# Down projection of a decoder block's FFN: from 528 plain matmuls to Strassen's seven products in two rounds

## The chip, the cores and the metric

The kernel runs on one core of one Trainium2 chip. The metric is the device time of one execution in microseconds, as the median of several runs of the same program. A run's time is a little more than the span of its profile, which goes from the first to the last instruction. The core has five engines that run beside each other, each through its own list of instructions in order: PE (matrix multiply), DVE (vector), ACT (scalar and activation functions), POOL (general purpose) and SP, which here issues DMAs. PE writes to PSUM, which has eight banks of 128 x 512 fp32.

## What is computed

One decoder block on 512 tokens of width 1024 in fp32: a mixing half (sliding-window attention beside a gated linear recurrence, merged by gates), then a SwiGLU FFN with 2816 hidden columns, each behind an RMS norm, and a last RMS norm. The change is in the FFN:

```python
u = rmsnorm(h, norm_ffn_g[layer])
z = (jax.nn.silu(jnp.einsum('bsd,df->bsf', u, w_ffn_gate[layer]))
     * jnp.einsum('bsd,df->bsf', u, w_ffn_up[layer]))
h = h + jnp.einsum('bsf,fd->bsd', z, w_ffn_down[layer])
return rmsnorm(h, norm_final_g)
```

## The kernel before, in words

**Arithmetic.** Every large product is done in three matmuls. Each operand is split into a high part, which is the value rounded to the type fp32r, and a low part, the rest; the product is high by high, high by low and low by high, summed in PSUM (lines 367 to 369 for projections, 886 for the down projection).

**Weights.** The class `Weights` (lines 41 to 117) streams all weights in one list of units. A unit is 1 MB: a tile `raw` of 128 x 2048, of which there are two buffers. Each unit makes two granules, `wh` and `wl` of 128 x 1024, with three buffers each. `split` has ACT copy a granule's high part (line 103) and DVE subtract it from the raw weights for the low part (line 107). `get` hands out the next granule and has the two behind it split. A raw buffer is loaded anew, through SP's queue, when the last subtraction that reads it is done.

**Before the FFN.** The output projection adds into `hn`, the residual stream: 4 token tiles of 128 rows by 1024 columns in SBUF (line 818). `hn` is transposed on PE into the PSUM tiles `px` (line 821), from which ACT and DVE make `u2h` and `u2l`, the split and transposed input of the FFN.

**Gate and up.** For each of the 11 pairs p of hidden tiles f (128 columns each) there are two gate products and two up products, each of 24 matmuls of 512 columns (tokens) into a PSUM tile `ps_f`. DVE multiplies the gate with the row scale `R` (line 855), ACT takes the sigmoid, POOL multiplies (lines 859 and 860), DVE multiplies the up product with the result to `zz` (line 865). ACT and DVE split it into `zh` and `zl` (lines 866 and 867). `R` itself comes from a small product into `ps_bc`, once, behind the first gate product (lines 255 to 261).

**Down.** For each of the 22 hidden tiles f, `z` of four token tiles is multiplied with the 128 x 1024 weights of f, into eight PSUM banks (two halves of 512 columns for each token tile). For the first 18 f the loop is over f, then token tiles. The weights of the last four f are all split ahead, and then the loop is over token tiles first: a token tile's sums are complete before the next one's last matmuls. So the end of row tile t (lines 897 to 929) runs beside the matmuls of t + 1: DVE adds `hn` (`residual`, line 907), ACT squares and sums, POOL multiplies by `gfin`, DVE reduces, POOL takes the power -0.5, ACT and DVE scale, and two DMAs write the row out.

**Order.** The program is recorded with a tile framework that puts each engine's instructions in an order of its own by a plan of when their inputs will be there; the order in the source is not always that of the engine. All waits are on semaphores.

Of the kernel before, what the change touches and what calls it, by code (L numbers as in the profile page):

```python
# [22 lines left out]
P = 128  # L23
# [10 lines left out]
TAIL_F = 4  # L34
# [6 lines left out]
class Weights:  # L41
# [13 lines left out]
    def load(self, u):  # L55
# [4 lines left out]
        if kind == "f":  # L60
# [23 lines left out]
    def split(self, i, pool=None, bufs=3, high=None, low=None, low_after=None):  # L84
# [5 lines left out]
        if kind == "c":  # L90
            src = raw.rearrange("p (k n) -> p k n", k=KD)[:, :, half * P:(half + 1) * P]
            shape = dict(k=KD)
        else:
            n = {"k": 256, "n": 512, "f": 1024}[kind]
            src = raw[:, half * 1024:(half + 1) * 1024].rearrange("p (k n) -> p k n", n=n)
            shape = dict(n=n)
        pool = pool or self.pool
        h = pool.tile([P, 1024], F32R, tag="wh", bufs=bufs, name=f"wh{i}")
        l = pool.tile([P, 1024], F32R, tag="wl", bufs=bufs, name=f"wl{i}")
        hv = h.rearrange("p (k n) -> p k n", **shape)  # L100
        lv = l.rearrange("p (k n) -> p k n", **shape)
# [7 lines left out]
        self.done = i + 1  # L109

# [10 lines left out]
def block_kernel(ctx: ExitStack, tc: tile.TileContext, x, norm_mix_g, w_in, b_in,  # L121
# [47 lines left out]
    for p in range(NF // 2):  # L169
        units += [("c", w_g, 256 * p), ("c", w_u, 256 * p)]  # L170
    units += [("f", w_d, 2 * p) for p in range(NF // 2)]
# [22 lines left out]
    reset = cst.tile([P, S], F32, name="reset")  # L194
    dve.memset(reset, 1.0)
    dve.memset(reset.rearrange("p (a b) -> p a b", b=64)[:, :, 0:1], 0.0)
    low_m = low.bitcast(U32).unsqueeze(1).broadcast_to([P, NT, P])
    up_m = up.bitcast(U32).unsqueeze(1).broadcast_to([P, NT, P])
# [39 lines left out]
    hib = cst.tile([P, D], F32, name="hib")  # L238
# [9 lines left out]
    uh = upool.tile([P, KD, S], F32R, name="uh")  # L248
    ul = upool.tile([P, KD, S], F32R, name="ul")
# [4 lines left out]

    def row_broadcast(dst, col, sp):
        diag = sp.tile([P, NT, P], F32, tag="diag", name="diag")
        for t in range(NT):
            dve.tensor_scalar(diag[:, t, :], ident, col[:, t:t + 1], None, ALU.mult)
        ps = ps1([P, S], "ps_bc")
        pe.matmul(ps, ones, diag.rearrange("p t c -> p (t c)"), start=True, stop=True)  # L260
        dve.tensor_copy(dst, ps)
# [574 lines left out]

    zpool = newpool("z", "right")
    fp = newpool("f", "right")
    zh = zpool.tile([P, NF, S], F32R, name="zh")
    zl = zpool.tile([P, NF, S], F32R, name="zl")  # L840

    def fproject(then=None):
        wh, wl = W.get(limit=len(W.grans) - 1 - TAIL_F)
        ps = psb([P, S], "ps_f")
        run(mm3(ps, wh, wl, u2h, u2l))
        if then:
            then()
        return ps

    for p in range(NF // 2):  # L850
        gs = []
        for a in range(2):
            zg = fp.tile([P, S], F32, tag="zg", bufs=2, name="zg")
            first = p == 0 and a == 0
            tt(zg, fproject((lambda: row_broadcast(R, rstd2, u2pool)) if first else None),  # L855
               R, ALU.mult)
            sg = fp.tile([P, S], F32, tag="sg", bufs=2, name="sgf")
# [3 lines left out]
            gs.append(zg)  # L861
        for a in range(2):
            f = 2 * p + a
            z = fp.tile([P, S], F32, tag="z", bufs=2, name="zz")
            tt(z, fproject(), gs[a], ALU.mult)  # L865
            act(zh[:, f, :], z, AF.Copy)
            tt(zl[:, f, :], z, zh.bitcast(F32)[:, f, :], ALU.subtract)
# [8 lines left out]
    acc0 = ps2([P, 2, S], "acc0")  # L876
    acc = [[acc0[:, 0, :], acc0[:, 1, :]],
           [ps1([P, S], "acc1"), ps1([P, S], "acc1")],
           [ps1([P, S], "acc2"), psb([P, S], "acc2")],
           [psb([P, S], "acc3"), psb([P, S], "acc3")]]  # L880

    def down(t, f, wh, wl, halves):
        ts = slice(t * P, (t + 1) * P)
        for ah, wv in ((zh, wh), (zh, wl), (zl, wh)):
            for half in halves:
                pe.matmul(acc[t][half], ah[:, f, ts], wv[:, 0, half * S:half * S + S],  # L886
                          start=f == 0 and ah is zh and wv is wh,
                          stop=f == NF - 1 and ah is zl)

    for f in range(NF - TAIL_F):  # L890
        wh, wl = W.get(limit=len(W.grans) - 1 - TAIL_F)
        for t in range(NT):
            down(t, f, wh, wl, (0, 1))
    first = len(W.grans) - TAIL_F
    for i in range(first, len(W.grans)):
        W.split(i, wd, TAIL_F)
    for t in range(NT):
        y = dp.tile([P, D], F32, tag="y", bufs=2, name="yo")
        jk = dp.tile([P, D], F32, tag="jk", bufs=1, name="jkd")
        s2 = dp.tile([P, 5], F32, tag="s2", bufs=2, name="s2d")  # L900
        dve.memset(s2[:, 4:5], EPS)

        def residual(half):
            for c in (2 * half, 2 * half + 1):
                cs = slice(c * 256, c * 256 + 256)
                o = (c % 2) * 256
                tt(y[:, cs], acc[t][half][:, o:o + 256], hn[:, t, cs], ALU.add)
                act(jk[:, cs], y[:, cs], AF.Square, scale=1.0 / 32.0,
                    accum_out=s2[:, c:c + 1])

        for half in range(2):
            for f in range(NF - TAIL_F, NF):
                down(t, f, *W.ready[first + f - (NF - TAIL_F)], (half,))
            if t:
                residual(half)
        if not t:
# [48 lines left out]
```

## Time and profile before

| | |
|---|---|
| median of 3 runs | 909.62 us (909.52 to 909.93) |
| profiled execution, its own time | 909.4 us |
| its span | 907.7 us |
| granted PE clock, mean | 0.999 |
| busy: PE, DVE, ACT, POOL | 896.5, 461.1, 368.2, 141.8 us |
| moved by DMA | 85.71 MB, mean 94 GB/s |
| stretch of the down projection's matmuls | 781.0 to 900.7 us |

In the profile's rows PE is the matmul, PEld its weight load, and L886 is line 886 of the kernel. A group's row has the line, the engine, the operation, what it writes and reads with the shapes, the number of instructions, then busy us and the mean ns of one, then the engine's idle time before them and what ended it. A row in order of time has start and length in us. A row of the table of windows has the stretch and its length, busy us with the number of instructions for PE, PEld, DVE, ACT and POOL, then the granted clock, the share of DMA and GB/s.

### The profile page before, as it was taken

To read this page: it belongs to the slowest core of one execution; us is meant where nothing else is said; L and a number is where in the kernel's file an instruction comes from. 1 tells how busy PE (TensorE), PEld (TensorE's weight loads), DVE (VectorE), ACT (ScalarE), POOL (GpSimd) and SP (SyncE) were. 2 spreads that over 40 slices of the span, in tenths; PEclk is the share of its full clock that TensorE was granted. 3 is DMA by queue.
4 is the path that set the end of the run, shared out by engine and by line. 5 is a ranking of instruction groups with operands and counts; after the bars stand their busy time and mean duration, and the time that the engine had idled before them with its cause. 6 is when DMAs were issued, how large, how long until landed. Compare 5 with 4: busy or idle time off the path is not lost.

```text
span 907.7 us, 11182 instructions
## 1 busy us (share of the span) xinstructions
PE 896.5 (99%) x4476; PEld 758.5 (84%) x4476; DVE 461.1 (51%) x717; ACT 368.2 (41%) x618; POOL 141.8 (16%) x148
## 2 busy tenths in 40 slices
PE   8999999999999999999999999999999999999996
PEld 7888889888898988888888887888888888888885
DVE  5677877647484755745335345344433344322314
ACT  6566765655453545215232333233222233211214
POOL 3013533300000000000000002222333322100004
PEclk9999999999999999999999999999999999999999
DMA  7221311222221141322243222222223333322212
GB/s 257 94 94 47 94 47 47 94 93 94 93 90 50 47 140 47 94 92 93 94 160 118 94 93 93 93 94 93 93 93 96 106 109 107 116 93 93 93 47 93
DMA packets 71472, 85.71 MB, mean 94 GB/s; under 512 B 1690, under 2 KB 64252, under 8 KB 71420
## 3 DMA queue, kind: packets, MB, share of 16 engines
q1 hardware_dynamic: 70828, 83.95, 28.5%
q10 hardware_dynamic: 592, 1.05, 0.3%
q8 instruction: 35, 0.57, 0.3%
q14 instruction: 17, 0.14, 0.0%
HBM read 82.90 MB, written 2.10 MB: 94 GB/s over the span
## 4 chain that ended last, share of the span: by engine, by line
PE 97%; SPq 1%; DMA 0%; DVE 0%; POOL 0%; ACT 0%; issue 0%; POOLq 0%; DVEq 0%
PE acc L886 13%; PE ps_big L367 13%; PE ps_big L369 13%; PE ps_big L368 13%; PE ps_f L368 9%; PE ps_f L369 9%; PE ps_f L367 9%; PE ps_v L378 2%; PE ps_v L379 2%; PE ps_v L377 2%; PE ps_o L379 2%; PE ps_o L378 2%; PE ps_o L377 2%; PE pv L503 1%; PE sc L447 1%; PE po L662 1%
## 5 line engine op out<-in xcount | busy, mean ns | idle before, releaser
L103 ACT ACTIVATE wh<-raw 128x1024 fp32r<-128x1024 f32 x147 | 155.1, 1059 | 401.3 <-PE ps_f L368 159.7
L107 DVE TENSOR_TENSOR wl<-raw,wh 128x1024 fp32r<-128x1024 f32 x147 | 180.5, 1230 | 163.7 <-ACT wh L103 163.5
L367 PE MATMUL ps_big<-uh,wh 128*128 128x512 f32 x376 | 148.8, 396 | 0.0
L368 PE MATMUL ps_big<-ul,wh 128*128 128x512 f32 x376 | 147.8, 393 | 0.0
L369 PE MATMUL ps_big<-uh,wl 128*128 128x512 f32 x376 | 147.7, 393 | 0.0
L368 PE MATMUL ps_f<-u2l,wh 128*128 128x512 f32 x352 | 137.5, 391 | 0.1
L367 PE MATMUL ps_f<-u2h,wh 128*128 128x512 f32 x352 | 137.0, 390 | 0.2 <-ACT u2h L134 0.2
L369 PE MATMUL ps_f<-u2h,wl 128*128 128x512 f32 x352 | 136.9, 389 | 0.0
L369 PEld LDWEIGHTS ps_big<-uh,wl 128*128 128x128 f32 x376 | 70.7, 188 | 14.2
L368 PEld LDWEIGHTS ps_big<-ul,wh 128*128 128x128 f32 x376 | 70.8, 188 | 13.6
L367 PEld LDWEIGHTS ps_big<-uh,wh 128*128 128x128 f32 x376 | 70.7, 188 | 13.5
L368 PEld LDWEIGHTS ps_f<-u2l,wh 128*128 128x128 f32 x352 | 66.1, 188 | 14.4 <-DVE u2l L827 0.5
L367 PEld LDWEIGHTS ps_f<-u2h,wh 128*128 128x128 f32 x352 | 66.0, 188 | 14.0 <-ACT u2h L134 0.5
L369 PEld LDWEIGHTS ps_f<-u2h,wl 128*128 128x128 f32 x352 | 66.1, 188 | 13.9 <-issue 0.2
L859 POOL TENSOR_TENSOR zg<-zg,sgf 128x512 f32<-128x512 f32 x22 | 39.4, 1794 | 162.6 <-ACT sgf L139 162.6
L886 PE MATMUL acc<-wh,zl 128*128 128x512 f32 x176 | 57.0, 389 | 0.0
L886 PE MATMUL acc<-wl,zh 128*128 128x512 f32 x176 | 56.9, 389 | 0.0
L886 PE MATMUL acc<-wh,zh 128*128 128x512 f32 x176 | 56.8, 389 | 0.0
L865 DVE TENSOR_TENSOR zz<-ps_f,zg 128x512 f32<-128x512 f32 x22 | 15.2, 692 | 66.4 <-PE ps_f L369 62.7
L855 DVE TENSOR_TENSOR zg<-ps_f,R 128x512 f32<-128x512 f32 x22 | 15.1, 691 | 62.6 <-PE ps_f L369 62.6
L253 POOL TENSOR_TENSOR r<-ss,neghalf 128x4 f32<-128x4 f32 x8 | 10.1, 1260 | 232.8 <-DVE ss L252 232.8
L886 PEld LDWEIGHTS acc<-wh,zh 128*128 128x128 f32 x176 | 33.0, 188 | 6.9
(222 smaller groups left out, 1478.1 us busy)
## 6 DMA issues: line engine op xcount, KB each, us to landing
raw<-in_w_in_dram SPq DMA_DIRECT2D x27, 1024.0 KB, 5.1
raw<-in_w_ffn_gate_dram SPq DMA_DIRECT2D x11, 1024.0 KB, 5.9
raw<-in_w_ffn_up_dram SPq DMA_DIRECT2D x11, 1024.0 KB, 5.2
raw<-in_w_ffn_down_dram SPq DMA_DIRECT2D x11, 1024.0 KB, 4.9
raw<-in_w_branch_attn_dram SPq DMA_DIRECT2D x4, 1024.0 KB, 5.3
raw<-in_w_branch_hgrn_dram SPq DMA_DIRECT2D x4, 1024.0 KB, 4.8
raw<-in_w_out_dram SPq DMA_DIRECT2D x4, 1024.0 KB, 5.5
xt<-in_x_dram SPq DMA_DIRECT2D x4, 512.0 KB, 6.5
```

The costliest lines, as they stand in the source:

```text
L103: nc.scalar.activation(hv, src, AF.Copy)
L107: (low or nc.vector).tensor_tensor(lv, src, hv.bitcast(F32), ALU.subtract)
L367: pe.matmul(ps, wh[:, k, :], ah[:, k, :], start=k == 0, stop=False)
L368: pe.matmul(ps, wh[:, k, :], al[:, k, :], start=False, stop=False)
L369: pe.matmul(ps, wl[:, k, :], ah[:, k, :], start=False, stop=k == KD - 1)
L377: pe.matmul(ps, ah[:, k0 + k, ts], wh[:, k, :], start=first and k == 0, stop=False)
L378: pe.matmul(ps, ah[:, k0 + k, ts], wl[:, k, :], start=False, stop=False)
L379: pe.matmul(ps, al[:, k0 + k, ts], wh[:, k, :], start=False, stop=last and k == nk - 1)
L855: tt(zg, fproject((lambda: row_broadcast(R, rstd2, u2pool)) if first else None), R, ALU.mult)
L859: pool_e.tensor_tensor(zg, zg, sg, ALU.mult)
L865: tt(z, fproject(), gs[a], ALU.mult)
L886: pe.matmul(acc[t][half], ah[:, f, ts], wv[:, 0, half * S:half * S + S], start=f == 0 and ah is zh and wv is wh, stop=f == NF - 1 and ah i ...
```

## The change

A product of two matrices, each in 2 x 2 blocks, is here made with seven block products instead of eight. The blocks of z are its token halves (256 tokens) by the two f of a pair; those of the down weights are the two f by the two halves of 512 output columns, `b11`, `b12` (first f), `b21`, `b22` (second f). Sums run over the 11 pairs. Each of the seven products of a pair is 2 token tiles x 3 terms = 6 matmuls of 512 columns.

**First round.** Three products (`n1y1`, `a12b21`, `n4b22`) go into six PSUM banks while gate and up still run: those of pair p - 1 stand between gate and up of pair p. Those of pair 9 and pair 10 come behind the last up product. The down weights of these pairs are loaded as units of kind `r1` among gate and up. DVE adds `b12` to `b11` in the raw buffer first, and three of the four blocks are split. z itself stays in a tile `z8` with eight slots of 256 columns: four blocks and four differences of them, made by DVE (lines 913 to 916 of the new kernel, L911 the eviction). Seven of the eight are split into `f1h` and `f1l` (first round) or `zh` and `zl` (second round, kept for all pairs).

**Between.** ACT copies the six banks to SBUF (`ev`), and POOL adds them into `hn`, eight additions of 512 columns (L957).

**Second round.** Four products (`a11b11`, `s3y3`, `s2y2`, `a22y4`) take all eight banks. The down weights are loaded a second time, as units of kind `r2`; DVE makes three sums of blocks in each raw buffer (L120) before the splits (L113). The weights of the last two pairs are split ahead. At the end the four products are combined: `a11b11` goes into all four row tiles, through a copy `v` made by ACT; `s2y2` completes rows 0 and 1; `s3y3` and `a22y4` complete rows 2 and 3. Each row tile then ends as before.

**Buffers.** PSUM is handed out anew at the start of the FFN: two banks for gate and up products (three before), six for the first round. `ps_bc` takes one of the two. The tiles `hib` and `reset` move to another pool.

The diff, cut to its core:

```diff
+    for p in range(NP):
+        ffn += [("g", p)] + ([("d", p - 1)] if 0 < p < NP - 1 else []) + [("u", p)]
+    ffn += [("d", NP - 2), ("d", NP - 1)]
...
+    units += [("r2", w_d, 2 * p) for p in range(NP)]
...
+    def sums(self, kind, half, raw):
+        b11, b12, b21, b22 = (raw[:, 512 * i:512 * i + 512] for i in range(4))
+        add = lambda o, i0, i1: self.nc.vector.tensor_tensor(o, i0, i1, ALU.add)
+        if kind == "r1":
+            if not half:
+                add(b11, b11, b12)
+        elif not half:
+            add(b12, b12, b22)
+        else:
+            add(b22, b11, b12)
+            add(b21, b21, b22)
...
+    def up_(p):
+        z8 = fp.tile([P, 8, 256], F32, tag="z8", bufs=1, name="z8")
+        n1, n4, a12, a11, s2, s3, a22, a21 = (z8[:, i, :] for i in range(8))
+        for a in range(2):
+            dst = z8.rearrange("p (a b) c -> p a b c", a=2)[:, :, 3 - a, :]
+            tt(dst, halves(fproject()), halves(gates_of[p][a]), ALU.mult)
+            if not a:
+                tt(s3, a21, a11, ALU.subtract)
+        tt(n1, a21, a22, ALU.subtract)
+        tt(s2, a11, n1, ALU.subtract)
+        tt(n4, a12, s2, ALU.subtract)
...
+        for h, l, src in ((h1, l1, z8[:, 0:3, :]), (zh[:, p], zl[:, p], z8[:, 3:7, :])):
+            act(h, src, AF.Copy)
+            tt(l, src, h.bitcast(F32), ALU.subtract)
...
+            act(ev, rounds1[n][i], AF.Copy)
+            for t, side in places:
+                dst = hn[:, t + i, sides[side]]
+                pool_e.tensor_tensor(dst, dst, ev, ALU.add)
...
+    for i in range(2):
+        p1 = tail("a11b11", i)
...
+        act(v, p1, AF.Copy)
+        add_side(i, 0, p1)
...
+    for i in range(2):
+        tt(vs[i], tail("s2y2", i), vs[i], ALU.subtract)
+        add_side(i, 1, vs[i])
+        finish_row(i, 1)
+    for i in range(2):
+        t = 2 + i
+        tt(vs[i], tail("s3y3", i), vs[i], ALU.add)
...
+        add_side(t, 1, vs[i])
+        tt(hn[:, t, 0:S], hn[:, t, 0:S], vs[i], ALU.subtract)
+    for i in range(2):
+        add_side(2 + i, 0, tail("a22y4", i))
+        finish_row(2 + i, 0)
```

**The order at three places.** Numbers in names tell buffers and granules apart: `wl146` is the low part of granule 146, `raw74` the raw tile of unit 74. Granules 144 to 147 are the first-round weights of pairs 9 and 10, and 148 is the first of the second round.

DVE at the end of the gate/up stream, from the eviction of the last up product on; before:

```order
L865 TENSOR_TENSOR zz_6278<-ps_f_6283,zg_6208 128x512
L107 TENSOR_TENSOR wl128_6331<-raw64_6244,wh128_6330 128x1024
L867 TENSOR_TENSOR zl_4762<-zz_6278,zh_4761 128x512
L901 MEMSET s2d_6860 128x1
L901 MEMSET s2d_6907 128x1
L107 TENSOR_TENSOR wl129_6359<-raw64_6244,wh129_6358 128x1024
L107 TENSOR_TENSOR wl130_6389<-raw65_6328,wh130_6388 128x1024
L107 TENSOR_TENSOR wl131_6417<-raw65_6328,wh131_6416 128x1024
```

and now:

```order
L911 TENSOR_TENSOR z8_6564<-ps_f_6603,zg_6529 128x2x256
L113 TENSOR_TENSOR wl146_6642<-raw73_6565,wh146_6641 128x512
L914 TENSOR_TENSOR z8_6564<-z8_6564 128x256
L120 TENSOR_TENSOR raw74_6638<-raw74_6638 128x512
L915 TENSOR_TENSOR z8_6564<-z8_6564 128x256
L120 TENSOR_TENSOR raw74_6638<-raw74_6638 128x512
L113 TENSOR_TENSOR wl147_6652<-raw73_6565,wh147_6651 128x1024
L916 TENSOR_TENSOR z8_6564<-z8_6564 128x256
L120 TENSOR_TENSOR raw74_6638<-raw74_6638 128x512
L921 TENSOR_TENSOR zl_4766<-z8_6564,zh_4765 128x1024
L113 TENSOR_TENSOR wl148_6671<-raw74_6638,wh148_6670 128x1024
L921 TENSOR_TENSOR f1l_6633<-z8_6564,f1h_6632 128x768
```

Where one eviction, a split of weights and a split of `zz` stood, the eviction is followed by three differences and three sums of weights, mixed with the splits; `n4` (L916) is the last input of `f1h`, and `f1l` stands twelfth.

DVE and POOL at the start of the second round. DVE from granule 149 on, where before the subtractions of the last three rows above went on alone:

```order
L113 TENSOR_TENSOR wl149_6683<-raw74_6638,wh149_6682 128x1024
L113 TENSOR_TENSOR wl150_6744<-raw75_6667,wh150_6743 128x1024
L120 TENSOR_TENSOR raw76_6740<-raw76_6740 128x512 x3
L113 TENSOR_TENSOR wl151_6762<-raw75_6667,wh151_6761 128x1024
L113 TENSOR_TENSOR wl152_6781<-raw76_6740,wh152_6780 128x1024
L113 TENSOR_TENSOR wl153_6799<-raw76_6740,wh153_6798 128x1024
L120 TENSOR_TENSOR raw77_6777<-raw77_6777 128x512 x3
L113 TENSOR_TENSOR wl154_6818<-raw77_6777,wh154_6817 128x1024
L113 TENSOR_TENSOR wl155_6836<-raw77_6777,wh155_6835 128x1024
```

POOL between the last gate (L899, L900; L859 and L860 before) and the end of the kernel; before:

```order
L859 TENSOR_TENSOR zg_6208<-zg_6208,sgf_6239 128x512
L860 TENSOR_TENSOR zg_6208<-zg_6208,R_4426 128x512
L920 TENSOR_TENSOR yo_6858<-yo_6858,gfin_6319 128x512
L920 TENSOR_TENSOR yo_6858<-yo_6858,gfin_6319 128x256
L924 TENSOR_TENSOR r1d_6898<-s1d_6896,neghalf_76 128x1
L920 TENSOR_TENSOR yo_6905<-yo_6905,gfin_6319 128x512
L920 TENSOR_TENSOR yo_6905<-yo_6905,gfin_6319 128x256
L924 TENSOR_TENSOR r1d_6945<-s1d_6943,neghalf_76 128x1
```

and now:

```order
L899 TENSOR_TENSOR zg_6529<-zg_6529,sgf_6560 128x512
L900 TENSOR_TENSOR zg_6529<-zg_6529,R_4426 128x512
L957 TENSOR_TENSOR hn_4420<-hn_4420,ev_6708 128x512 x2
L957 TENSOR_TENSOR hn_4420<-hn_4420,ev_6712 128x512 x2
L957 TENSOR_TENSOR hn_4420<-hn_4420,ev_6716 128x512
L957 TENSOR_TENSOR hn_4420<-hn_4420,ev_6719 128x512
L957 TENSOR_TENSOR hn_4420<-hn_4420,ev_6722 128x512
L957 TENSOR_TENSOR hn_4420<-hn_4420,ev_6725 128x512
L1010 TENSOR_TENSOR hn_4420<-hn_4420,gfin_6706 128x512 x2
L1010 TENSOR_TENSOR hn_4420<-hn_4420,gfin_6706 128x256 x2
L1014 TENSOR_TENSOR r1d_7133<-s1d_7131,neghalf_76 128x1
L1014 TENSOR_TENSOR r1d_7157<-s1d_7155,neghalf_76 128x1
```

On DVE the sums of the next unit (`raw76`) now stand ahead of the second split of the unit before it (`wl151`). On POOL, eight additions into `hn` stand between the last gate and the multiplies by `gfin` (L1010), which came as two for each row before.

PE at the end; before, from the last matmuls of a half row on:

```order
L886 MATMUL acc3_6326<-wh147_6854,zh_4761 128x512
L886 MATMUL acc3_6326<-wl147_6855,zh_4761 128x512
L886 MATMUL acc3_6326<-wh147_6854,zl_4762 128x512
L886 MATMUL acc3_6327<-wh144_6842,zh_4761 128x512
L886 MATMUL acc3_6327<-wl144_6843,zh_4761 128x512
L886 MATMUL acc3_6327<-wh144_6842,zl_4762 128x512
L886 MATMUL acc3_6327<-wh145_6846,zh_4761 128x512
L886 MATMUL acc3_6327<-wl145_6847,zh_4761 128x512
L886 MATMUL acc3_6327<-wh145_6846,zl_4762 128x512
L886 MATMUL acc3_6327<-wh146_6850,zh_4761 128x512
```

and now, from the last matmul of the first `a11b11` on (four more of `a22y4` follow):

```order
L982 MATMUL a11b11_0_6732<-wh168_7074,zl_4766 128x512
L982 MATMUL a11b11_1_6733<-wl168_7075,zh_4765 128x512
L982 MATMUL a11b11_1_6733<-wh168_7074,zl_4766 128x512
L982 MATMUL s3y3_0_6734<-wl168_7075,zh_4765 128x512
L982 MATMUL s2y2_0_6736<-wl169_7081,zh_4765 128x512
L982 MATMUL s2y2_0_6736<-wh169_7080,zl_4766 128x512
L982 MATMUL s2y2_1_6737<-wl169_7081,zh_4765 128x512
L982 MATMUL s2y2_1_6737<-wh169_7080,zl_4766 128x512
L982 MATMUL s3y3_0_6734<-wh168_7074,zl_4766 128x512
L982 MATMUL s3y3_1_6735<-wl168_7075,zh_4765 128x512
L982 MATMUL s3y3_1_6735<-wh168_7074,zl_4766 128x512
L982 MATMUL a22y4_0_6738<-wl169_7081,zh_4765 128x512
```

Before, one bank's matmuls stand together and a row is complete long before the end; now the last matmuls of all eight banks stand among each other, and the first bank is complete 15 matmuls before the last. At the start of the FFN, PE now has all 16 transposes `px` ahead of the first gate product; before, 23 matmuls of two gate products stood between the first eight and the other eight.

More of the change, by code (lines that the diff above doesn't have):

```diff
@@ L33 @@
     1024, 1152, 1280, 2304, 3328, 4352, 5376, 6400)
-TAIL_F = 4
+NP = NF // 2
+TAIL_P = 2
 WARM = 28
@@ L93, in split @@
         else:
-            n = {"k": 256, "n": 512, "f": 1024}[kind]
+            n = 256 if kind == "k" else 512
             src = raw[:, half * 1024:(half + 1) * 1024].rearrange("p (k n) -> p k n", n=n)
             shape = dict(n=n)
+        size = 1024
+        if kind in ("r1", "r2"):
+            self.sums(kind, half, raw)
+            if kind == "r1" and not half:
+                src, size = src[:, 0:1, :], 512
         pool = pool or self.pool
@@ L890, in block_kernel @@
[L890 to L900, printed above, removed]
-        dve.memset(s2[:, 4:5], EPS)
[L903 to L916, printed above, removed]
-            residual(0)
-            residual(1)
-        for hs in (slice(0, S), slice(S, S + 256)):
```

170 lines of the change are left out of this document (116 added, 54 removed).

## The prediction

> **What bounds the kernel now.** I read the page first: engine shares, then the chain that ended last.
>
> ```profile
> PE 896.5 (99%) x4476; PEld 758.5 (84%) x4476; DVE 461.1 (51%) x717; ACT 368.2 (41%) x618; POOL 141.8 (16%) x148
> ...
> PE 97%; SPq 1%; DMA 0%; DVE 0%; POOL 0%; ACT 0%; issue 0%; POOLq 0%; DVEq 0%
> ```
>
> PE is the path for 97% of the span, so a matmul taken away is worth its whole spacing, and any wait put before PE costs its whole length. The chain of waits for the last stage gives the spacing and the tail, and the table of windows how busy the others are beside it.
>
> ```profile
> 781.01 119.69 PE acc L886 x528
> ...
> 900.73 0.43 DVE yo L907
> ...
> 901.19 0.52 ACT jkd L134 x2
> ...
> 901.77 0.57 POOL yo L920
> ...
> 903.04 0.35 DVE yo L926
> ```
>
> ```profile
> 780.90:900.90 120.00, 119.79 (x529) 98.87 (x527) 34.68 (x50) 29.91 (x52) 8.82 (x10) 1.00 0.26 92
> 900.90:907.70 6.80, 0.00 (x0) 0.00 (x0) 1.49 (x5) 1.63 (x5) 1.38 (x3) 0.86 0.20 78
> ```
>
> The down projection is 528 matmuls in 119.69 us without a hole: 0.2267 us each. Its last ends at 900.70, and the span ends at 907.7: a tail of 7.0 us, in which one half row goes once through DVE, ACT, POOL, DVE and out. DVE is busy for 34.68 of 120 us, ACT for 29.91, POOL for 8.82: no one but PE is late.
>
> The costs of the other engines come from the groups by shape, the DMA issues (their last number is us to landing) and DVE's last operations in order of time (start, length).
>
> ```profile
> L107 DVE TENSOR_TENSOR wl<-raw,wh 128x1024 fp32r<-128x1024 f32 x147 | 180.5, 1230 | 163.7 <-ACT wh L103 163.5
> L103 ACT ACTIVATE wh<-raw 128x1024 fp32r<-128x1024 f32 x147 | 155.1, 1059 | 401.3 <-PE ps_f L368 159.7 <-PE ps_big L368 130.3 <-PE acc L886 62.4
> L860 POOL TENSOR_TENSOR zg<-zg,R 128x512 f32<-128x512 f32 x22 | 28.3, 1289 | 1.6
> L867 DVE TENSOR_TENSOR zl<-zz,zh 128x512 fp32r<-128x512 f32 x22 | 15.1, 684 | 0.0
> L134 ACT ACTIVATE zh<-zz 128x512 fp32r<-128x512 f32 x22 | 13.9, 631 | 1.2 <-DVE zz L865 1.2
> L907 DVE TENSOR_TENSOR yo<-acc,hn 128x256 f32<-128x256 f32 x16 | 5.9, 417 | 16.8 <-PE acc L886 16.8
> ```
>
> ```profile
> raw<-in_w_ffn_gate_dram SPq DMA_DIRECT2D x11, 1024.0 KB, 5.9
> ...
> raw<-in_w_ffn_down_dram SPq DMA_DIRECT2D x11, 1024.0 KB, 4.9
> ...
> raw<-in_w_in_dram SPq DMA_DIRECT2D x4, 512.0 KB, 6.6
> ```
>
> ```profile
> 900.73 0.76 DVE L907 TENSOR_TENSOR yo<-acc,hn 128x256 f32<-128x256 f32 x2 [1.70 <-PE acc L886]
> 902.13 0.16 DVE L922 TENSOR_REDUCE s1d<-s2d 128x1 f32<-128x5 f32 x1 [0.64 <-ACT jkd L134]
> 903.04 0.35 DVE L926 TENSOR_SCALAR yo<-yo,r1d 128x256 f32<-128x256 f32 x1 [0.75 <-POOL r1d L924]
> 903.31 0.48 DVE L927 SCALAR_TENSOR_TENSOR yo<-yo,r1d,gfin 128x256 f32<-128x256 f32 x1
> ```
>
> Two of 256 columns take 0.76, so 0.34 each in a row; the others likewise lose some 0.09: 0.60 for 512, 1.14 for 1024.
>
> **Matmuls.** Eleven pairs of f by seven products, two token tiles and three terms are 462 matmuls, against 528. 66 by 0.2267 is -15.0 us. That PE's order holds 462 rules out that the change does not do what it says.
>
> **Inside the stream: 0.** Moving three products there only moves PE time. A pair now takes 48 + 48 + 18 matmuls, 25.8 us. DVE's work in it is 14.2 us (five subtractions of weights at 1.23 and one at 0.69, one sum of weights, four evictions, four differences at 0.42, two splits at 1.23 and about 0.96), 55%. The three loads, in SP's queue between those of gate and up, have 25.8 us for three landings of 5 to 6. A product waits for forms made a whole gate (10.9 us) before it. Two PSUM buffers in place of three leave 5.4 us for an eviction of 0.7. Without that cover, each microsecond late would cost one. The moves of hib and reset change nothing that is issued before the seam below.
>
> **The seam before the stream: +1.2.** PE and DVE there, in order of time:
>
> ```profile
> 537.93 1.23 DVE L107 TENSOR_TENSOR wl<-raw,wh 128x1024 fp32r<-128x1024 f32 x1 [4.48 <-ACT wh L103]
> 539.07 1.28 DVE L818 TENSOR_TENSOR hn<-ps_o,hn 128x512 f32<-128x512 f32 x2
> ...
> 548.25 0.69 DVE L261 COPY R<-ps_bc 128x512 f32<-128x512 f32 x1
> ```
>
> ```profile
> 538.00 1.03 PE L821 MATMUL px<-ident,hn 128*128 128x128 f32 x8
> 538.79 0.48 PE L367 MATMUL ps_f<-u2h,wh 128*128 128x512 f32 x1
> ...
> 544.90 0.48 PE L369 MATMUL ps_f<-u2h,wl 128*128 128x512 f32 x1
> 545.60 0.73 PE L367 MATMUL ps_f<-u2h,wh 128*128 128x512 f32 x2 [0.21 <-ACT u2h L134]
> 546.38 0.50 PE L368 MATMUL ps_f<-u2l,wh 128*128 128x512 f32 x1
> 546.73 0.40 PE L369 MATMUL ps_f<-u2h,wl 128*128 128x512 f32 x1
> ```
>
> Before, PE fills the wait for hn with two gate products (from 538.79). Now all 16 transposes stand ahead of the first product: four wait for the first hn (539.76, a hole of 1.0), four for the second (540.35, 0.2). Then the second gate product takes ps_bc's buffer and waits for the copy to R: 0.69 and a little, 0.9. Before, the four starts from 544.90 to 546.73 took 1.83 in place of 0.91: 0.9 of waits that go. 2.1 - 0.9 = +1.2 (bounds 0.3 to 2.1).
>
> **The last pair: +2.0.** Let E be the end of the last up product. Pair 9's 18 matmuls cover 4.08 us. In that time DVE must run what its order shows up to n4: evict (0.60), subtract weights (0.60), n1 (0.34), sum (0.60), s2 (0.34), sum (0.60), subtract weights (1.14), n4 (0.42): 4.64. ACT is then still on wh148, which waited for pair 9's last matmul, until 4.08 + 0.17 + 1.06 = 5.3; f1h, 768 columns, lies between 0.63 and 1.06, say 0.85. PE goes on at E + 6.1: a wait of 2.0. If raw74's landing holds the sums up, it is more (to 3.5); at best 0.9.
>
> **The start of round two: +6.5, of which 4.6 from POOL.** Two pairs of views decide it, first DVE and POOL where both want their inputs from SBUF, then DVE on PSUM beside POOL:
>
> ```profile
> 559.95 1.70 DVE L107 TENSOR_TENSOR wl<-raw,wh 128x1024 fp32r<-128x1024 f32 x1
> ```
>
> ```profile
> 558.02 2.53 POOL L860 TENSOR_TENSOR zg<-zg,R 128x512 f32<-128x512 f32 x2
> ```
>
> ```profile
> 888.79 1.52 DVE L927 SCALAR_TENSOR_TENSOR yo<-yo,r1d,gfin 128x256 f32<-128x256 f32 x1
> ...
> 892.82 0.48 DVE L927 SCALAR_TENSOR_TENSOR yo<-yo,r1d,gfin 128x256 f32<-128x256 f32 x1
> ...
> 895.29 0.76 DVE L907 TENSOR_TENSOR yo<-acc,hn 128x256 f32<-128x256 f32 x2 [1.33 <-PE acc L886]
> ```
>
> ```profile
> 888.64 1.39 POOL L920 TENSOR_TENSOR yo<-yo,gfin 128x512 f32<-128x512 f32 x1 [0.16 <-ACT jkd L134]
> ...
> 894.69 1.30 POOL L920 TENSOR_TENSOR yo<-yo,gfin 128x512 f32<-128x512 f32 x1 [2.17 <-ACT jkd L134]
> ```
>
> The subtraction that usually takes 1.23 took 1.70 when it began inside a POOL multiply that ended at 560.55; the operation of 0.48 took 1.52, ending 0.28 after POOL. DVE's 0.76 on PSUM beside POOL's 1.30 was not touched. So a DVE operation with two SBUF inputs and a POOL operation on SBUF run one after the other. The Trainium skill says so too ("SBUF — State Buffer", section "Who interferes with whom": the second to issue is blocked until the first is through); the trace agrees, 1.70 against 1.23.
>
> Now POOL gets eight additions of 1.29 into hn just when DVE has the sums and splits of the first weights, all of them with two SBUF inputs. In us after E: pair 10 runs on PE to 10.2, then w148 to 12.9. raw75 is issued when wl147 is done (4.7) and lands at 9.6; its sums end at 11.7, when POOL starts. wl149 gets in at 13.0 and ends at 14.1 (PE wanted it 1.0 earlier); POOL; wl150; raw76, issued at 14.2, lands at 19.0. Then three sums, with a POOL addition in between each time and one after (0.65 + 1.25 each, 5.7), and wl151, which DVE's order has behind them, ends at 25.8. PE has used up w150 and wants it at 20.3: a wait of 5.5, with the first 6.5. If nothing blocked, wl151 would end at 21.1 and the wait be 1.9. ACT's six copies out of the first round's banks (0.54 each) run in pair 10's and w148's time, and gfin's load goes out between raw75 and raw76: nothing for either. From there PE sets the pace: 24 matmuls, 5.4 us a pair, against 4.1 us of DVE, and two raw buffers that turn in 4.9 + 4.3 against 10.9.
>
> A hole of 5.5 us may also cost clock: the window after the last matmul shows 0.86 over 6.8 us, that is 1.9 us at half, from some 4.9 us after it. No row shows how fast it comes back; between 0 and 2.5, I take +0.7. The Trainium skill ("TensorE: Matmul & The Clock Gate", Part 1) puts the idle window at about 3.4 us; by an estimate from that page the hole would lose up to 1.7; the drop 4.9 us after the last matmul agrees with it as far as it goes.
>
> **The tail: +12.4.** In PE's order the first a11b11 stops 15 matmuls, 3.4 us, before the end X, and all four rows' sums hang behind it; before, each row's sums began when its own products were through, and only the last half row was left at X. DVE, after ACT's copy to v (0.63), has 16 operations of 256 (5.4), six of 512 (3.6), and a reduction, a scaling and a last product for each row (0.16 + 0.27 + 0.40, 3.3): 12.3 from X - 2.7, so X + 9.6, and 1.4 for the last squares and POOL: X + 11.0. Before, the last output was issued at X + 3.1 (903.31 + 0.48). +7.9. POOL's four multiplies of 1.3 and four of 0.7 hold 8.0 us in the same stretch, beside DVE's additions of v and last products, all two SBUF inputs: between 0 and 8.0; I take 4.5, as about half of DVE's time there is on such operations.
>
> **Sum.** -15.0 + 1.2 + 2.0 + 6.5 + 0.7 + 12.4 = +7.8. The profiled execution took 909.4 (span 907.7 and 1.7 around it), so 917.2; the runs' median, 909.62, is 0.2 above it: **917.4 us**.
>
> **The rivals.** *POOL and DVE do not exclude each other* (the other side): one mechanism, in the two places above. 4.6, 0.7 and 4.5 go: -2.0, 907.6, faster. It turns when less than 2.0 of those 9.8 remain. Against it stand the four rows above; for it, that few such collisions are in the trace. 0.10, and 0.09 for a part of it (908 to 912). *Loads land late*: round two asks for 1 MB every 5.4 us where 10.9 was usual; at 5.9 to 6.6 a landing the three in series (raw74, 75, 76) add 3 to 5: 920 to 923. 0.13. *All covers hold and the tail is as before*: 909.6 - 15.0 + 1.2 = 895.8. Nothing in the orders speaks for it. 0.05. *My forecast*, 912 to 921: 0.63.
>
> A measurement tells about 0.2% (1.8 us) from no change. Faster: 0.05, and nearly all of the 0.10: 0.15. Same: 0.07. Slower: 0.78. The range runs from 907.5, the edge of the POOL rival, to 922, which takes in most of the late landings.
>
> **What would show it.** 462 matmuls of the down projection at 0.2267; a hole of some 2 us before the last pair's products; wl151 late by about 5 us, with additions of POOL between DVE's sums; the last matmul near 896 and the span's end some 19 us behind it. I am wrong if DVE's sums keep their 0.69 beside POOL, if the tail after the last matmul is under 12 us, or if PE shows holes of several microseconds elsewhere.

## The result, and the profile after

| | before | after |
|---|---|---|
| time, median of 4 runs (us) | 909.76 (909.52 to 909.93) | 918.50 (918.00 to 919.07) |
| ratio to before | | 1.0096, 95% interval 1.0079 to 1.0114 |
| the profiled execution: time, span (us) | 909.4, 907.7 | 919.07, 917.2 |
| last matmul ends, span's end behind it (us) | 900.7, 7.0 | 899.1, 18.1 |

The change takes 66 matmuls away and makes the kernel slower by 8.7 us; 917.4 was forecast. The page of the changed kernel, the engine shares, the shares of the chain that ended last, and the two groups of DVE that grew:

```profile
PE 885.4 (97%) x4410; PEld 747.8 (82%) x4410; DVE 554.4 (60%) x833; ACT 398.3 (43%) x648; POOL 163.1 (18%) x156
...
PE 89%; DVE 4%; DMA 3%; SPq 1%; issue 1%; ACT 0%; POOL 0%; POOLq 0%; DVEq 0%; ACTq 0%
...
L113 DVE TENSOR_TENSOR wl<-raw,wh 128x1024 fp32r<-128x1024 f32 (+1 forms) x169 | 211.6, 1253 | 112.0 <-ACT wh L109 111.7
...
L120 DVE TENSOR_TENSOR raw<-raw 128x512 f32<-128x512 f32 x44 | 33.7, 765 | 38.8 <-DMA raw<-in_w_ffn_down_dram 38.1
```

PE has 66 instructions and 11 us less than before, and its share of the chain falls from 97% to 89%: DVE and the loads now stand in it. Where, the table of windows shows (time busy and number of instructions of PE, PEld, DVE, ACT and POOL, then the granted clock, the DMA share, GB/s):

```profile
825.25:839.30 14.05, 13.46 (x57) 10.60 (x58) 9.86 (x13) 5.88 (x9) 8.79 (x6) 1.00 0.53 184
839.30:845.30 6.00, 0.41 (x3) 0.01 (x1) 5.93 (x5) 2.11 (x2) 4.85 (x3) 0.92 0.00 0
845.30:851.20 5.90, 5.90 (x14) 4.64 (x15) 3.09 (x4) 0.06 (x1) 0.00 (x0) 0.50 0.84 285
...
899.10:917.20 18.10, 0.02 (x1) 0.00 (x0) 13.79 (x28) 8.05 (x29) 9.76 (x12) 0.59 0.30 116
```

For 6 us PE does almost nothing while DVE is full and POOL is busy for 4.85; then PE runs for 5.9 us at half clock; and 18.1 us follow the last matmul. PE's waits from the transposes ahead of the FFN on, in order of time (the bracket is the idle time ahead of the row and what ended it; the row of ps_bc has none):

```profile
539.84 1.26 PE L839 MATMUL px<-ident,hn 128*128 128x128 f32 x8 [0.78 <-DVE hn L836]
...
546.42 1.02 PE L879 MATMUL ps_bc<-diag,ones 128*128 128x512 f32 x2
548.22 0.50 PE L385 MATMUL ps_f<-u2h,wh 128*128 128x512 f32 x1 [0.78 <-DVE R L880]
...
825.20 0.50 PE L928 MATMUL n1y<-wh,f1h 128*128 128x512 f32 x1 [1.96 <-ACT f1h L153]
...
833.29 0.50 PE L928 MATMUL s2y<-wl,zh 128*128 128x512 f32 x1 [0.59 <-DVE wl L113]
...
845.29 0.79 PE L928 MATMUL s2y<-wl,zh 128*128 128x512 f32 x1 [5.59 <-DVE wl L113]
```

The column counts from the modelled end of the matmul before. Between starts, less the usual 0.23, the three waits of the down projection are 2.1, 0.75 and 5.74 us; in the text they are given so. DVE beside the longest of them:

```profile
830.95 2.29 DVE L113 TENSOR_TENSOR wl<-raw,wh 128x1024 fp32r<-128x1024 f32 x1
...
838.14 4.89 DVE L120 TENSOR_TENSOR raw<-raw 128x512 f32<-128x512 f32 x3 [2.67 <-DMA raw<-in_w_ffn_down_dram]
842.95 4.55 DVE L113 TENSOR_TENSOR wl<-raw,wh 128x1024 fp32r<-128x1024 f32 x3
```

and POOL, all eight additions in one row:

```profile
830.51 13.64 POOL L957 TENSOR_TENSOR hn<-hn,ev 128x512 f32<-128x512 f32 x8 [17.15 <-ACT ev L153]
```

The split of w149 takes 2.29 in place of 1.22, three sums 4.89 in place of 2.14, and POOL's additions 1.7 each in place of 1.29: they take turns. w151, the first of the last row, is through at about 845.2. The tail, on DVE:

```profile
896.46 0.76 DVE L1001 TENSOR_TENSOR hn<-a11b,hn 128x256 f32<-128x256 f32 x2 [4.52 <-ACT v L153]
...
898.99 3.15 DVE L1001 TENSOR_TENSOR hn<-v,hn 128x256 f32<-128x256 f32 x4
...
905.93 1.35 DVE L1016 TENSOR_SCALAR hn<-hn,r1d 128x256 f32<-128x256 f32 x1
907.20 1.48 DVE L1017 SCALAR_TENSOR_TENSOR hn<-hn,r1d,gfin 128x256 f32<-128x256 f32 x1
```

and on POOL beside it:

```profile
897.96 3.56 POOL L1010 TENSOR_TENSOR hn<-hn,gfin 128x512 f32<-128x512 f32 x3 [53.80 <-issue]
...
905.42 2.98 POOL L1010 TENSOR_TENSOR hn<-hn,gfin 128x512 f32<-128x512 f32 x2 [0.87 <-ACT jkd L153]
```

DVE begins 2.7 us before the last matmul's end and has no pause until 910.9. Four additions of v take 3.15 in place of 1.4, and a scaling and a last product take 1.35 and 1.48 beside POOL's multiplies, where 0.34 and 0.47 are usual.

The seam before the stream is measured at the 96th matmul of the first gates, where both kernels run without a hole again; in before:

```profile
563.03 0.39 PE L367 MATMUL ps_f<-u2h,wh 128*128 128x512 f32 x1
```

and in after:

```profile
564.45 0.39 PE L387 MATMUL ps_f<-u2h,wl 128*128 128x512 f32 x1
```

So 1.4 us were lost there. (The two rows have other names, as the order within a product differs; both are the 96th.) From there to the last up product the stream takes 254.32 us in place of 217.60: its 162 additional matmuls' own time and nothing more.

### The profile page after: what moved, and what is told of

Read it like the earlier page. It is cut to its first block, busy times and chain, and to the rows that moved or that the text cites. A ratio compares the mean times of both kernels' runs of the same rounds, so it can differ in the third digit from the quotient of the medians.

```text
span 917.2 us, 11242 instructions
## 1 busy us (share of the span) xinstructions
PE 885.4 (97%) x4410; PEld 747.8 (82%) x4410; DVE 554.4 (60%) x833; ACT 398.3 (43%) x648; POOL 163.1 (18%) x156
## 4 chain that ended last, share of the span: by engine, by line
PE 89%; DVE 4%; DMA 3%; SPq 1%; issue 1%; ACT 0%; POOL 0%; POOLq 0%; DVEq 0%; ACTq 0%
PE ps_big L385 13%; PE ps_big L386 13%; PE ps_big L387 13%; PE ps_f L385 8%; PE ps_f L387 8%; PE ps_f L386 8%; DMA raw<-in_w_ffn_down_dram 3%; PE ps_v L396 2%; PE ps_v L397 2%; PE ps_v L395 2%; PE ps_o L396 2%; PE ps_o L397 2%; PE ps_o L395 2%; PE pv L521 1%; PE n4b L928 1%; PE a12b L928 1%
## 5 line engine op out<-in xcount | busy, mean ns | idle before, releaser
L109 ACT ACTIVATE wh<-raw 128x1024 fp32r<-128x1024 f32 (+1 forms) x169 | 174.0, 1032 | 372.8 <-PE ps_f L386 145.9
L113 DVE TENSOR_TENSOR wl<-raw,wh 128x1024 fp32r<-128x1024 f32 (+1 forms) x169 | 211.6, 1253 | 112.0 <-ACT wh L109 111.7
L899 POOL TENSOR_TENSOR zg<-zg,sgf 128x512 f32<-128x512 f32 x22 | 37.9, 1723 | 194.2 <-ACT sgf L158 194.2
L120 DVE TENSOR_TENSOR raw<-raw 128x512 f32<-128x512 f32 x44 | 33.7, 765 | 38.8 <-DMA raw<-in_w_ffn_down_dram 38.1
L911 DVE TENSOR_TENSOR z<-ps_f,zg 128x512 f32<-128x512 f32 x22 | 15.1, 688 | 37.9 <-PE ps_f L387 37.9
L900 POOL TENSOR_TENSOR zg<-zg,R 128x512 f32<-128x512 f32 x22 | 36.7, 1669 | 1.7
L395 PE MATMUL ps_v<-wh,uh 128*128 128x256 f32 x128 | 36.5, 285 | 0.0
L396 PE MATMUL ps_v<-wl,uh 128*128 128x256 f32 x128 | 36.3, 284 | 0.0
L397 PE MATMUL ps_v<-wh,ul 128*128 128x256 f32 x128 | 36.2, 284 | 0.0
```

The costliest lines, as they stand in the source:

```text
L109: nc.scalar.activation(hv, src, AF.Copy)
L113: (low or nc.vector).tensor_tensor(lv, src, hv.bitcast(F32), ALU.subtract)
L120: add = lambda o, i0, i1: self.nc.vector.tensor_tensor(o, i0, i1, ALU.add)
L395: pe.matmul(ps, ah[:, k0 + k, ts], wh[:, k, :], start=first and k == 0, stop=False)
L396: pe.matmul(ps, ah[:, k0 + k, ts], wl[:, k, :], start=False, stop=False)
L397: pe.matmul(ps, al[:, k0 + k, ts], wh[:, k, :], start=False, stop=last and k == nk - 1)
```

## The experiments

The theory after the result: the sum's terms stand where I put them, and POOL's work beside DVE's is the largest of them; what I had mis-sized is the clock. The rivals: the loads, or the order of DVE's work, hold w151; the clock falls for another reason; the end is bound by the last products. Each run stands beside runs of the kernel before on the same chip (909.61 and 909.82 in the two groups); gains are against after's 918.50.

**Without the first round's additions.**

```
-                pool_e.tensor_tensor(dst, dst, ev, ALU.add)
+                if n == "none":
+                    pool_e.tensor_tensor(dst, dst, ev, ALU.add)
```

(The condition is never true.)

> Leaves out POOL's eight additions of the first round's products to hn (the output lacks those products); everything else, ACT's six copies out of the banks too, stays. Theory (POOL blocks DVE at the start of round two, and the hole then costs clock): the hole of 0.75 us before w149's matmuls goes, the sums of the third pair of f take 2.1 us in place of 4.9 and their load is issued 1.1 us earlier, so that the split w151 ends some 4 us earlier and the hole before its matmuls falls from 5.74 to 1.5 to 1.9 us; with so short a hole the clock stays at 1.00, which gives back the 3.2 us that 17 matmuls at 0.43 cost. 0.75 + 4.0 + 3.2 = 8.0: 910.5 us (909.5 to 911.5). Rival (the loads, or the order of DVE's work alone, hold w151): the hole stays over 4.5 us, the clock falls to 0.50 behind it, and the time stays within 1.5 us of 918.5.

Measured: 912.04 us (911.37 to 912.74, ten runs), ratio 1.0023 (1.0013 to 1.0033); the profiled execution took 911.37. PE's wait at w151:

```profile
840.33 0.50 PE L928 MATMUL s2y<-wl,zh 128*128 128x512 f32 x1 [1.45 <-DVE wl L113]
```

DVE there:

```profile
836.99 2.15 DVE L120 TENSOR_TENSOR raw<-raw 128x512 f32<-128x512 f32 x3 [1.87 <-DMA raw<-in_w_ffn_down_dram]
839.05 3.49 DVE L113 TENSOR_TENSOR wl<-raw,wh 128x1024 fp32r<-128x1024 f32 x3
```

The sums take 2.15, their load lands 1.1 us earlier, the wait is 1.6 (1.84 between starts), and that of w149 is gone: of 6.5 us POOL had caused 4.9. The clock stays at 1.00 in this profile, which is 7.7 us shorter than after's, against 8.0 expected. The median of the runs is 6.5 shorter, so the time lies 0.5 us above the range expected; the runs spread over 1.4 us. The rival fell.

**Matmuls of zeros in the long hole.**

```
+    zeros = dp.tile([P, P], F32R, name="zeros")
+    act(zeros, ident, AF.Copy, scale=0.0)
...
+                with tc.issue_after(raw_ins(last)):
+                    for k in range(12):
+                        last = pe.matmul(acc["a11b11"][k % 2], zeros, wh[:, k % 2],
+                                         start=False, stop=False)
...
```

(The matmuls of that pair that stand ahead of the hole and behind it are taken out of the loop, so that they keep their places around the zeros.)

> Nothing is taken away: PE gets 12 more matmuls, of a block of zeros, at the place of the long hole before w151's matmuls (2.7 us of work that adds nothing), so the 5.74 us without a matmul become 2.8 to 3.0 us without one, and the time at which w151 is there stays. Theory (the half clock from 844.3 to 851.2 us is the price of PE's idleness): the clock stays at 1.00 behind the hole, 3.2 us come back, less up to 0.4 for the order of what follows: 915.5 us (915.0 to 916.2). Rival (the clock falls for another reason, as the load on the memory or the other engines at that place): 17 matmuls at 0.43 stay, 918.2 to 919.0.

Measured: 916.26 us (three of four runs 916.02 to 916.48, one 918.79), ratio 1.0076 (1.0060 to 1.0092). 2.2 us are won, not 3.0; the median lies just above the range expected, and the slowest of the runs in the rival's. The clock did fall, for one stretch in place of two. The windows of this run:

```profile
840.59:844.01 3.42, 1.40 (x7) 0.82 (x5) 3.42 (x3) 1.06 (x1) 3.42 (x3) 1.00 0.00 0
844.01:847.42 3.41, 3.41 (x8) 2.72 (x9) 3.23 (x2) 0.00 (x0) 1.01 (x1) 0.50 0.66 219
847.42:850.80 3.38, 3.38 (x16) 2.74 (x15) 1.47 (x3) 0.68 (x1) 0.00 (x0) 1.00 0.91 318
```

and those of after:

```profile
840.94:844.35 3.41, 0.00 (x0) 0.00 (x0) 3.38 (x3) 1.06 (x1) 3.21 (x2) 1.00 0.00 0
844.35:847.76 3.41, 2.47 (x6) 1.99 (x7) 3.16 (x3) 0.00 (x0) 0.00 (x0) 0.50 0.42 92
847.76:851.18 3.42, 3.42 (x10) 2.64 (x9) 0.87 (x2) 0.04 (x1) 0.00 (x0) 0.50 1.01 398
851.18:854.60 3.42, 3.42 (x17) 2.79 (x16) 2.89 (x4) 2.08 (x2) 0.00 (x0) 1.00 0.31 123
```

But the run changes more than PE's idleness. ACT now makes `zeros` ahead of its copies out of the banks, which come 0.2 us later, and raw75 lands 0.3 us earlier, so POOL's first addition (830.69) begins after w149's split and not before it; the split takes 1.22 again, PE's wait for it is gone, and w151's matmuls begin at 843.95 in place of 845.29:

```profile
830.61 1.22 DVE L113 TENSOR_TENSOR wl<-raw,wh 128x1024 fp32r<-128x1024 f32 x1
...
843.95 0.77 PE L988 MATMUL s2y<-wl,zh 128*128 128x512 f32 x1 [2.02 <-DVE wl L113]
```

The clock changes only at the ends of fixed stretches of 3.41 us (last section). One begins at 844.01, just behind PE's restart, so the first slow stretch is full and the clock comes back behind it; in after the first slow stretch was in part empty. Without the zeros the stretch from 840.59 would have been empty, as in after, and by the same stretches the clock would have fallen and come back at the same times. The 1.7 us that the half clock costs here are also no less than in the runs below whose hole of 5.7 us is untouched (1.7 to 2.7). So this run does not show that work on PE shortens the slow time, and it does not decide between theory and rival. What speaks for PE's idleness as the cause is the 16 falls in the ten traces, in the last section. (My expectation counts 17 slow matmuls and 3.2 us; three of them are first starts behind other holes. It is 14, and 2.9 us.)

**The last 48 matmuls in the order of their sums.**

```
+    for n in ("a11b11", "s2y2"):
+        for i in range(2):
+            tail(n, i, (NP - 2,))
...
-        p1 = tail("a11b11", i)
+        p1 = tail("a11b11", i, (NP - 1,))
...
+                with tc.issue_after(chain[0]) if chain[0] else nullcontext():
```

> The last 48 matmuls are put in the order of the sums that hang behind them: a11b11 and s2y2 of the tenth pair of f, then of the eleventh, then s3y3, then a22y4. The first a11b11 then stops some 12 to 15 matmuls into the tail, at about 891.5 us, in place of 895.5. Theory (the tail is DVE's chain from the first stop): all of DVE's work moves up by 4.0 us and the span's end with it; the last matmul stays at 899.1: 914.5 us (913.5 to 915.5), 14 us behind the last matmul in place of 18.1. Rival (the last row's own products and sums bound the tail, as in the kernel before): under 1 us.

Measured: 914.22 us (914.17 to 914.67), ratio 1.0048 (1.0033 to 1.0063). DVE's first addition and the time behind the last matmul:

```profile
891.65 0.76 DVE L1010 TENSOR_TENSOR hn<-a11b,hn 128x256 f32<-128x256 f32 x2 [0.47 <-ACT v L153]
...
898.40:912.50 14.10, 0.00 (x0) 0.00 (x0) 9.73 (x22) 6.08 (x20) 6.71 (x9) 0.57 0.39 149
```

DVE begins 4.8 us earlier, and the tail is 14.1 us in place of 18.1: the theory's 4.0. The rest is the last matmul's own, which ends 0.7 us earlier here, mainly as the half clock costs 1.8 us in place of 2.9. The rival fell.

**Without the last multiplies on POOL.**

```
         for hs in (early, ls):
-            pool_e.tensor_tensor(y[:, hs], y[:, hs], gfin[:, hs], ALU.mult)
+            if t > 3:
+                pool_e.tensor_tensor(y[:, hs], y[:, hs], gfin[:, hs], ALU.mult)
```

(The four rows are t = 0 to 3, so the condition is never true.)

> Leaves out POOL's eight multiplies of the last rows by the final norm's gain (the output lacks that gain in three quarters of its columns). Theory (POOL's multiplies block DVE in the tail, with the clock and the start unchanged): the operations that took 3.15, 1.35, 1.48, 1.40 and 0.81 us there take about 1.4, 0.27, 0.48, 1.36 and 0.35, so 4.0 to 4.5 us go: 914.2 us (913.5 to 915.0). Rival (POOL's work lies beside DVE's and ACT's squares set the pace): under 1 us.

Measured: 915.03 us (914.90 to 915.31), ratio 1.0057 (1.0042 to 1.0072). The last matmul ends at 898.8, 14.5 us before the end: the tail is 3.6 us shorter, a little less than expected, and the time lies at the upper edge of its range; DVE now waits twice, 0.66 us each, for POOL's r1, which it did not in after. The rival fell.

**The additions on DVE, one a pair.**

```
-                dst = hn[:, t + i, sides[side]]
-                pool_e.tensor_tensor(dst, dst, ev, ALU.add)
+                later.append((hn[:, t + i, sides[side]], ev))
...
+        if p >= 1:
+            with tc.issue_after(W.low_ins):
+                dst, ev = later.pop(0)
+                tt(dst, dst, ev, ALU.add)
```

> The eight additions of the first round's products stay, but DVE makes them, one behind the last split of each pair from the second to the ninth of round two, where a pair leaves DVE 1.3 us of 5.4 (8 x 0.60 us). Theory (POOL's block at the start of round two, not the work as such): the profile is that of the run without the additions, one hole of 1.6 to 1.9 us before w151's matmuls: 912.0 us (911.3 to 912.8). Rival (the additions cost wherever they stand): DVE falls behind PE and 2 us or more of the 6.5 are not won: 914 us or more.

Measured: 912.06 us (911.86 to 912.67, ten runs), ratio 1.0026 (1.0016 to 1.0035): the time of the run that leaves them out, to 0.02 us. One wait stays, as there:

```profile
840.42 0.50 PE L929 MATMUL s2y<-wl,zh 128*128 128x512 f32 x1 [1.39 <-DVE wl L113]
```

The work is free on DVE where DVE has room; on POOL at that place it cost 6.4 us. The edit changes both the engine and the time of the additions; whether POOL could also have made them one a pair for nothing was not run.

**v left in the banks.**

```
-        tt(vs[i], tail("s2y2", i), vs[i], ALU.subtract)
-        add_side(i, 1, vs[i])
+        p2 = tail("s2y2", i)
+        tt(p2, p2, vs[i], ALU.subtract)
+        act(vs[i], p2, AF.Copy)
+        add_side(i, 1, p2)
...
-        tt(vs[i], tail("s3y3", i), vs[i], ALU.add)
+        p3 = tail("s3y3", i)
+        tt(p3, p3, vs[i], ALU.add)
+        vs[i] = p3
```

> In the tail the differences and sums with v are left in the banks of s2y2 and s3y3, so that the ten operations that add them to hn read one operand from PSUM and one from SBUF; two copies by ACT of 0.6 us are added, POOL's multiplies stay. Theory (only a DVE operation with two SBUF operands waits for POOL): the four additions that took 3.15 us take 1.4, and POOL, which also waited, is through earlier: 1.8 to 4.2 us, 914.3 to 916.7, I take 915.3. Rival (POOL blocks DVE whatever its operands' place): no difference, 918.0 to 919.0.

Measured: 914.62 us (914.10 to 915.52), ratio 1.0053 (1.0038 to 1.0068). The additions that took 3.15 for four, on DVE and now from the bank:

```profile
897.77 0.75 DVE L1001 TENSOR_TENSOR hn<-s2y,hn 128x256 f32<-128x256 f32 x2
...
899.03 0.74 DVE L1001 TENSOR_TENSOR hn<-s2y,hn 128x256 f32<-128x256 f32 x2
```

POOL multiplies beside them (898.23 to 900.87 in its own row of the trace), and they take their usual 0.33 each. The tail is 15.0 us (897.9 to 912.9): 3.1 us won there with POOL's work still in place, nearly what leaving it out wins. Another 1.2 lie ahead of the last matmul in this profile, where the half clock happened to begin earlier and met 3.4 us of matmuls in place of 5.9; the medians differ by 3.9 in all. The rival fell.

**The last pair's forms first.**

```
+        ins = tt(n4, a12, s2, ALU.subtract)
+        formed[p] = raw_ins(ins)
...
+            late = p == NP - 2 and len(names) == 2 or p == NP - 1
+            with tc.issue_after(formed[NP - 1]) if late else nullcontext():
+                wh, wl = W.get(limit=stream_end)
```

> DVE makes the last pair's forms ahead of the sums and splits that stood between them, and nothing else is moved by hand. Theory (what follows is held by DVE and the loads, not by PE): the hole of 2.1 us before the last pair's products goes to 0.3, and PE then waits longer at the next places; of the 1.9 us 0.5 to 1.2 are left at the end: 917.6 us (916.6 to 918.4, with the clock's own spread). Rival (the terms of my sum add up): 1.9 us go: 916.6 or less, with the holes at w149 and w151 as they were.

Measured: 915.77 us (915.12 to 916.73), ratio 1.0066 (1.0051 to 1.0081): 2.7 us, more than either expected. PE's waits:

```profile
824.42 0.50 PE L929 MATMUL n1y<-wh,f1h 128*128 128x512 f32 x1 [0.17 <-ACT f1h L153]
832.44 0.50 PE L929 MATMUL s2y<-wl,zh 128*128 128x512 f32 x1 [0.48 <-DVE wl L113]
838.05 0.50 PE L929 MATMUL a11b<-wl,zh 128*128 128x512 f32 x1 [1.88 <-DVE wl L113]
843.65 0.62 PE L929 MATMUL s2y<-wl,zh 128*128 128x512 f32 x1 [2.56 <-DVE wl L113]
```

My theory fell: the first hole went and little was given back, since the scheduler, with the forms placed, also put one of the three sums behind the next split. The hole of 5.7 became two of 2.0 and 2.7, the holes together fell from 8.6 to 5.7, and the slow clock lasted one stretch, not two. The rival has the direction, but not its reason, for the holes did not stay as they were. How much is the forms' and how much the sums' order, this run cannot say.

**All of it together.** To the four edits above (additions, tail's order, v, forms) come two: a pair's three sums are made together, behind both splits of the pair before it, and the broadcast of `R` goes into a bank of the first round in place of one of gate and up.

```
         elif not half:
             add(b12, b12, b22)
-        else:
             add(b22, b11, b12)
             add(b21, b21, b22)
...
+            W.sums_after = tc.issue_after(W.low_ins) if p >= 1 else None
...
-    bc = psg("ps_bc")
+    bc = rounds1["n4b22"][1]
```

> All that the theory points to, with the output complete: first-round additions on DVE, one a pair; the last pair's forms first; each pair's three sums behind both splits of the pair before it; the broadcast of the norm's factor in a bank of its own; the last 48 matmuls in the order of their sums; v in the banks. Theory: 11 to 12 us of PE's holes and slow clock go, so the last matmul ends at 887 to 888, and the span's end comes 11 to 12 us behind it in place of 18: 900.5 us (899 to 903). Rival (with the holes gone, loads of 4.9 us and DVE's 4.7 us a pair no longer fit PE's 5.44 us and a wait comes in every pair): over 905 us.

Measured: 901.04 us (900.54 to 901.34), ratio to before 0.9901 (0.9885 to 0.9918): faster than both kernels, by 8.8 us than before and 17.5 than after. Its engine shares on the page:

```profile
PE 882.9 (98%) x4410; PEld 746.7 (83%) x4410; DVE 551.2 (61%) x841; ACT 399.1 (44%) x650; POOL 150.1 (17%) x148
```

and its windows from the start of round two on:

```profile
829.00:888.50 59.50, 59.50 (x263) 48.94 (x261) 55.64 (x76) 29.48 (x49) 4.73 (x6) 1.00 0.48 160
888.50:899.40 10.90, 0.04 (x1) 0.00 (x0) 5.82 (x17) 5.05 (x16) 5.79 (x7) 0.73 0.50 193
```

PE has no hole in 59.5 us, with DVE busy for 55.6 of them; the last matmul ends 10.9 us before the end. The rival fell, though with 94% DVE has hardly anything left there.

## Why the prediction was right

The time was 1.1 us over the forecast, inside the range, with the sign forecast. Step by step, in us of the profiled execution:

| step | forecast | measured | by |
|---|---|---|---|
| 66 matmuls fewer | -15.0 | -15.0 | 462 at 0.2267 |
| inside the stream | 0 | 0.0 | trace of after |
| the seam | +1.2 | +1.4 | 96th matmul |
| the last pair | +2.0 | +2.1 | trace of after |
| start of round two | +6.5 | +6.5 | trace of after |
| of it POOL | 4.6 | 4.9 | run without the additions |
| clock behind the hole | +0.7 | +2.9 | 14 matmuls at 0.43 |
| first starts behind holes | not counted | about +0.5 | what is left to 899.1 |
| the tail | +12.4 | +11.1 | 18.1 against 7.0 |
| of it POOL | 4.5 | 3.1 to 3.6 | runs with v in the banks, and without the multiplies |
| sum | +7.8 | +9.5 | 917.2 against 907.7 |

**Right for the reason given:** the start of round two. That DVE with two SBUF operands and POOL run one after the other was argued from four rows of before; the rows above, and three runs, show it. The rival that they do not exclude each other fell, and so did that of late loads: the 22 loads land in 4.9 us.

**Mis-sized: the clock.** "Between 0 and 2.5, I take +0.7" was too low at both the value and its upper end. I had the onset from before's tail but no row for the return. It is the return that costs: a stretch at half clock in which PE is again idle for a large part (2.47 of 3.41 us busy in after) did not end it, so two of 3.41 us followed a hole of 5.7. The size is also a matter of luck: the same hole of 5.7 us cost 2.9 us in after's trace, 2.7 in that without the multiplies, 1.8 in that with the tail in order and 1.7 in that with v in the banks, by where it fell against the stretches. The last two lie inside the bounds.

**Mis-sized the other way: the tail.** The last matmul came 3.0 us later than the 896.1 of the sum, the tail was 1.3 us shorter than forecast. POOL's share was 1 us less than my half of DVE's time, and the first a11b11 stopped at 895.7, 3.4 before the end, as the order had said. In total the two errors add 0.9 us, so that the sum came as near as it did is in part luck: they have opposite signs. The rest of the 1.9 by which the profiled execution (919.07) passed the 917.2 forecast for it lies in the seam, in the last pair, in the starts behind holes and, with 0.2, outside the span.

**The terms were less separate than a sum has it.** Closing the hole before the last pair won 2.7 us where its term was 2.0, as the later holes, the order of the sums and the clock moved with it; the four edits run alone win 6.4, 4.3, 3.9 and 2.7, 17.3 together, and all six at once 17.5.

## What to carry to other kernels

Work moved from the busiest engine is paid where the other engines' new work piles up: here at one place, eight additions given to an idle POOL just when DVE's splits fed PE cost 4.9 us of waits and, in the one trace, 2.9 us of clock (6.4 us between the medians), and the same additions one a pair on DVE cost nothing. Before DVE and POOL are given work side by side, count the operands that each reads from SBUF; leaving one in the bank that it came from took the conflict away. And at the end of a kernel put the matmuls in the order in which the chain behind them begins, with the sum that most others hang on first.

## What the runs showed of the hardware

**The clock goes by fixed stretches of 3.41 us.** In all ten traces the changes of PE's granted clock lie a whole number of stretches of 3.413 us apart (4.67, 844.35, 851.18 and 902.38 in after: 246, 2 and 15). Each of the 16 falls in the ten traces comes at the end of such a stretch in which PE had worked for 0 to 1.42 us, and no such stretch at full clock is without a fall behind it. Here, from the run with the tail in order, one stretch that was not followed by a fall and one that was:

```profile
822.01:825.42 3.41, 1.47 (x7) 0.89 (x5) 3.41 (x7) 2.91 (x3) 0.00 (x0) 1.00 0.11 12
839.07:842.49 3.42, 0.97 (x5) 0.47 (x3) 3.35 (x3) 1.06 (x1) 3.42 (x3) 1.00 0.00 0
```

With 1.47 busy the clock stayed, with 1.42 (at the end of the run with zeros, 895.21 to 898.62, where the matmuls are the kernel's own) it fell. Behind a hole it went up again only after a stretch that was full; 2.47 of 3.41 in after was not enough. Less than full can do: at the start of after, PE's matmuls of 128 columns came every 0.21 us up to 4.67 and every 0.11 behind it, and the stretch that ended there held 2.81 us of work. So what a hole costs depends on where in the stretches it falls: one of 2.7 us cost clock in the run with the last pair's forms first, one of 2.1 before the last pair in none of the profiles that have it. Whether matmuls of zeros count as work for the clock no run shows. The Trainium skill says in "TensorE: Matmul & The Clock Gate", Part 1, that the window is free-running and 3413 ns long; the traces agree. It has the fall after an idle window; here a window that was 42% busy (1.42 of 3.41) was enough. That the start of the stretches against the program also makes the runs of one kernel spread (1.4 us over ten runs without the additions) fits this but was not shown, since only one run of each kernel has a trace; the mean clock on record for each run gives no clear answer (0.993 for the two fastest without the additions, 0.989 to 0.992 for the other eight, but also 0.993 for one of the slower runs, 912.57, with the additions on DVE).

**A scaling waits for POOL too.** The operation L1016, one tensor and a column from SBUF, took 1.35 us beside POOL's multiply in place of 0.34 (0.35 at the same place in the run without the multiplies); I had counted only operations with two tensors. The Trainium skill ("SBUF — State Buffer", section "Who interferes with whom") names such scalings among the operations that can contend with POOL; the trace agrees.
